# A streaming encoder layer on one core: down product's first operands loaded into the up stage's raw weight places, inverse roots issued in two parts, gate rows loaded further ahead

## The chip, the core and the metric

The kernel runs on one core of a Trainium2 chip. Five engines work side by side, each through its own queue in order: TensorE (PE, matmuls, with its weight loads as PEld), VectorE (DVE), ScalarE (ACT), GpSimd (POOL) and SyncE (SP). SP here only issues DMAs; POOL issues others, mostly those that add into memory. The metric is the device time of one execution in microseconds, the median of several runs.

## The reference, cut to what matters

One layer runs on 1024 prompt and 32 sample tokens (T = 1056) with width 1024. Between two mixing branches and the end stand the two parts in which the change lies:

```python
# ConvFFN: DFF = 2816
a, g = split(rms(x) @ w_up)
f    = (gelu(conv3(g)) * a) @ w_down
x    = x + rms(f) * g_post_ffn
# per-layer embedding
gate = sigmoid((rms(x) * g_pre_ple) @ w_ple_gate)
x    = x + rms(gate * (p @ w_ple)) * g_post_ple
```

## The kernel before, in words

Everything is kept transposed: features lie on the 128 partitions, tokens along the free axis. A product in nearly full fp32 is three matmuls in a reduced format: weights and rows are each split into a high part (an ACT copy, tiles `whi`, `d0` to `d8`, `eh`) and a low part (a DVE subtraction, `wlo`, the same `d` tiles, `el`), and hi·hi, hi·lo and lo·hi are added up.

**Up stage.** `up_strassen(f)` makes feature tile f (4 to 21) of the up product with seven half-size products (`mul`). It loads two raw weight tiles: one into the pool `wp` (tag `raw`, two places), one into the pool `sw` (tag `sraw`, two places). The pools `mp` and `sp` hold the normalised rows (`mh`, `ml`, and their sums `t1`, `t2`); `t3` lies in `sw`. For the last tile, f = 21, the final DVE steps are kept in a function `ends`, called later as `last_up[2]()`. `activate_steps` applies convolution and gelu and POOL writes the result to DRAM, `d_b`.

**Down product.** Seven products p, each of four output groups m; u = 4p + m counts groups from 0 to 27. One group is 11 tiles k of weights against rows, in three parts q (k 0 to 3, 4 to 7, 8 to 10), each k with two column halves and three matmuls: 66 matmuls. `row_load(p, i)` brings rows k = 2i and 2i+1 from `d_b` into a place `uraw` (three places), `row_split(p, i)` splits them into a `d` tile; `w_load(u)` brings a group's weights into a place `wraw` (two places), `w_split(u, q)` splits one part into `whi` and `wlo` (four places each). `uraw` and `wraw` are in the pool `rp`, which lies where `ml` was; the `d` tiles lie where `mh`, `ml` and the sums were. `gate_ahead` loads (into `raw`) and splits the gate's weights between the groups, from u = 4 on, and writes them to `d_gate`.

While products 5 and 6 run, `norm_first` does the norms of the first half of the tokens (`one`) in steps, at the places that `NORM_1` names: sums of squares, `inverse` (1/sqrt by ACT's Ln and Exp and one Newton step on DVE), `norm_rows`, and `norm_split`, which makes the gate's row tiles `eh` and `el`. `square_sum` gathers squares for the second half at the same time.

**Gate stage.** Products (c, n): c = 0 is the first half of the tokens in two column parts j, c = 1 and 2 are the quarters; n counts 8 output tiles. After each product's 24 matmuls ACT takes a sigmoid out of PSUM (`sig`), DVE multiplies it with a row of `d_pl` that SP has loaded into `plt` (L1759, L1769), ACT squares it, DVE adds the square up. `norm_second` does the second half's norms in steps at the places of `NORM_2`; `LAST` says where the last norm's total, sum, `inverse` and rows of quarters 0 and 1 stand. Each `inverse` needs another ACT function table than the sigmoid, so it is preceded and followed by an ACT_TABLE_LOAD. The last quarter's own norm follows all products: three pairs of matmuls with `onesM` (L1850), Ln, Exp, DVE, and the writes of `y`.

**What sets the order.** From the down product on PE, DVE and ACT keep the order in which the code is written (`manual_schedule`); what an engine waits for holds up all that stands behind it. SP's and POOL's queues are ordered by the scheduler, and an issue that waits for its place to be read holds up the issues behind it. The names with L are lines of the profile.

Of the kernel before, what the change touches and what calls it, by code (L numbers as in the profile page):

```python
# [112 lines left out]
def emit(tc, a):  # L113
# [1067 lines left out]

    def up_strassen(f):
        raw = [tl(wp, [P, KT, P], tag="raw", bufs=2), tl(wp, [P, KT, P], tag="raw", bufs=2) if f == UP_PLAIN else tl(sw, [P, KT, P], tag="sraw", bufs=2)]
# [48 lines left out]
        if f == FT - 1:  # L1232
# [6 lines left out]
            mul(Z, weight(s4, WL_ENG[5]), "b22", True, True)  # L1239
            ac.activation(c12, Z_, AF.Copy)  # L1240
# [9 lines left out]
            s3 = plus(a11, a21, ALU.subtract, WS_ENG[2])  # L1250
# [91 lines left out]
    def row_load(p, i):  # L1342
        if p < len(RSRC):
            n = 2 if i < 5 else 1
            raws[p, i] = tl(rp, [P, 2, HT], tag="uraw", bufs=3)[:, :n]
            dma.dma_start(raws[p, i], d_b[RSRC[p], 2 * i : 2 * i + n].rearrange("k p t -> p k t"))
# [36 lines left out]
    def w_load(u):  # L1383
        if u < NU:
            t = tl(rp, [P, HD * P], tag="wraw", bufs=2)
            dma.dma_start(t, WSRC[u // 4][u % 4])
            wraw[u] = t.rearrange("p (k c) -> p k c", c=P)

    def w_split(u, q):
        if u < NU:  # L1390
            raw, n = wraw[u][:, KS[q] : KS[q + 1]], KS[q + 1] - KS[q]
# [71 lines left out]
    def inverse(out, parts):  # L1463
# [5 lines left out]

        for ps, s in parts:  # L1470
            ac.activation(like(y, ps, s), ps, AF.Ln)
        ac.activation(y, y, AF.Exp, scale=-0.5)
        ve.tensor_tensor(t, y, y, op=ALU.mult)
        for ps, s in parts:
            ve.scalar_tensor_tensor(like(t, ps, s), like(t, ps, s), -0.5, ps, op0=ALU.mult, op1=ALU.mult)
        ve.scalar_tensor_tensor(out, t, 1.5, y, op0=ALU.add, op1=ALU.mult)
# [32 lines left out]
    def norm_split(s, rs, eh, el):  # L1509
        zs = pairs_of(s)  # L1510

        def low_half(i):
            ve.tensor_tensor(el[:, 2 * i : 2 * i + 2], zs[i], eh[:, 2 * i : 2 * i + 2], op=ALU.subtract)
# [8 lines left out]
        low_half(i)  # L1522
        yield
# [4 lines left out]
    def norm_first():  # L1528
# [5 lines left out]
        log_exp()  # L1534
        rs = tl(np_, [P, HT], tag="rs", bufs=1)
        inverse(rs, parts)
# [6 lines left out]
        log_exp()  # L1543
        rs = tl(np_, [P, HT], tag="rs", bufs=1)
        inverse(rs, parts)
# [5 lines left out]
    def norm_second():  # L1551
# [3 lines left out]
        log_exp()  # L1555
        rs = tl(np_, [P, HT], tag="rs", bufs=1)
        inverse(rs, parts)
        yield
# [7 lines left out]
        def tail(j, hl):  # L1566
            parts = own_sums(*hl)
            log_exp()
            r2 = tl(np_, [P, HC], tag="r2", bufs=1)
            inverse(r2, parts)  # L1570
            yield
# [34 lines left out]
    def gate_weights(n):  # L1606
# [8 lines left out]
        else:  # L1615
            if n < 4:
                t = [tl(rp, [P, HD * P], F32R, tag="wraw", bufs=2) if n == 2 else tl(rp, [P, 2, HT], F32R, tag="uraw", bufs=3).rearrange("p k t -> p (k t)") for x in range(2)]
# [20 lines left out]
    norm = None  # L1638
    for u in range(NU):
# [3 lines left out]
        for q in range(3):  # L1643
# [42 lines left out]
            if u == NU - 1 and q:  # L1686
                gate_weights(q - 1)
                gate_weights(q + 1)
            for i in range(NORM_1.get((p, m, q), 0)):
                next(norm, None)  # L1690
            if (p, m, q) in SQUARES_2:
# [3 lines left out]
                square_sum(acc[1], i, z[:, 4 + 2 * i : 6 + 2 * i, two])  # L1695
# [7 lines left out]
        if p == 6 and m % 2:  # L1703
            square_sum(acc[1], 2 + m // 2, z[:, m - 1 : m + 1, two])
# [4 lines left out]
        if (p, m) == (5, 3):  # L1709
            ub.release()  # L1710
    for i in norm:
        pass
# [19 lines left out]
    def last_inverse(c):  # L1732
        log_exp()
        w = SETS[c].stop - SETS[c].start
        rs = tl(np_, [P, HT], tag="rs", bufs=1)[:, :w]
        inverse(rs, sums[c])
# [212 lines left out]
```

## Time and profile before

| | us |
|---|---|
| median of 3 runs | 1987.55 |
| the runs | 1986.78 to 1989.57 |
| the profiled execution, its own time | 1986.21 |
| its span, first to last instruction | 1984.5 |
| PE busy in the span | 1929.8 (97%) |
| DVE busy | 1251.3 (63%) |
| ACT busy | 951.5 (48%) |
| POOL busy | 407.6 (21%) |
| granted TensorE clock, mean | 0.992 |

The profile is of one execution; times in it count from the span's start. A row of the timeline has start, duration, engine, line, operation, output<-input, shape and count, and in brackets how long the engine had been idle before and what ended that. A row of waits says which engine and line waited for which, the sum, the number of times and the longest. A row of windows has, for a stretch, its length, then each engine's busy time with its count of instructions (PE, PEld, DVE, ACT, POOL), the granted clock, the share of the DMA engines and their GB/s. In this trace the up stage ends and the down product begins near 1626, the gate stage begins near 1866, and the last gate product ends near 1961.5.

### The profile page before, as it was taken

Reading aid. Unit: us, or ns where it says so; the run is one execution under the profiler, and the core shown is the slowest. Engines: PE = TensorE matmul, PEld = TensorE weight load, DVE = VectorE, ACT = ScalarE, POOL = GpSimd, SP = SyncE. Lnnn points to the kernel's source line nnn. Section 1 sums busy time; section 2 is a strip of 40 time slices with the busy share of each in tenths; the row PEclk is TensorE's granted clock in tenths of the full one; section 3 lists DMA queues with packets and bytes.
Section 4 is the critical chain, followed back from the end, with each engine's and each line's share of the span. In section 5 each row is a group of like instructions: output and inputs, shape, how many; then the busy total and the mean of one; then the engine's idle time right before and its main releaser. Section 6 shows DMA issues by size and latency. Waiting matters only on the chain.

```text
span 1984.5 us, 34506 instructions
## 1 busy us (share of the span) xinstructions
PE 1929.8 (97%) x13594; PEld 1889.1 (95%) x13594; DVE 1251.3 (63%) x2546; ACT 951.5 (48%) x1747; POOL 407.6 (21%) x470
## 2 busy tenths in 40 slices
PE   8999999999999999998999999999999989999996
PEld 7999999999999999998999999999999989999995
DVE  7556556466376485466644676877677765558775
ACT  6356455454364553663423454434333344555554
POOL 4423322243122131111120121111112111001102
PEclk9999999999999999999999999999999999999998
DMA  7212211266235261337744256544445568887646
GB/s 281 68 56 75 72 56 57 71 173 176 85 105 143 92 170 60 107 107 234 277 132 136 89 160 214 174 130 136 130 114 119 115 172 281 271 289 245 224 124 107
DMA packets 106861, 289.04 MB, mean 146 GB/s; under 512 B 11652, under 2 KB 33868, under 8 KB 106060
## 3 DMA queue, kind: packets, MB, share of 16 engines
q1 hardware_dynamic: 78780, 198.45, 31.2%
q0 software_dynamic: 27632, 88.04, 16.3%
q8 instruction: 106, 1.74, 0.4%
q14 instruction: 55, 0.45, 0.1%
q10 hardware_dynamic: 288, 0.36, 0.1%
HBM read 198.49 MB, written 111.39 MB: 156 GB/s over the span
## 4 chain that ended last, share of the span: by engine, by line
PE 77%; DVE 12%; ACT 5%; DMA 4%; issue 3%; SPq 0%; POOL 0%; DVEq 0%; ACTq 0%
PE mm L228 13%; PE mm L229 13%; PE mm L230 13%; PE two L1209 6%; PE two L1211 6%; PE two L1210 6%; PE two L1652 2%; PE two L1651 2%; PE two L1650 2%; PE one L508 2%; PE two L730 2%; PE one L466 1%; DVE d L698 1%; DMA ev<-d_inv 1%; DMA uraw<-d_b 1%
## 5 line engine op out<-in xcount | busy, mean ns | idle before, releaser
L228 PE MATMUL mm<-xh,whi 128*128 128x352 f32 x1248 | 412.3, 330 | 0.0
L230 PE MATMUL mm<-xh,wlo 128*128 128x352 f32 x1248 | 412.1, 330 | 0.0
L229 PE MATMUL mm<-xl,whi 128*128 128x352 f32 x1248 | 410.0, 329 | 0.0
L208 POOL TENSOR_TENSOR wlo<-raw,whi 128x512 fp32r<-128x512 f32 x130 | 185.2, 1433 | 681.3 <-ACT whi L207 628.7
L228 PEld LDWEIGHTS mm<-xh,whi 128*128 128x128 f32 x1248 | 235.5, 189 | 1.6 <-DVE ev L352 0.5
L229 PEld LDWEIGHTS mm<-xl,whi 128*128 128x128 f32 x1248 | 235.2, 188 | 1.7 <-issue 0.3
L230 PEld LDWEIGHTS mm<-xh,wlo 128*128 128x128 f32 x1248 | 234.8, 188 | 1.1
L1650 PE MATMUL two<-d,whi 128*128 128x264 f32 x616 | 176.0, 286 | 4.2 <-ACT whi L1394 2.9
L1652 PE MATMUL two<-d,wlo 128*128 128x264 f32 x616 | 176.6, 287 | 2.1 <-DVE wlo L1395 2.0
L1651 PE MATMUL two<-d,whi 128*128 128x264 f32 x616 | 175.7, 285 | 2.9 <-DVE d L1354 2.9
L207 ACT ACTIVATE whi<-raw 128x512 fp32r<-128x512 f32 (+1 forms) x146 | 89.4, 621 | 157.0 <-PE mm L229 94.1
L1211 PE MATMUL two<-mh,wlo 128*128 128x264 f32 x576 | 163.1, 285 | 0.0
L1210 PE MATMUL two<-ml,whi 128*128 128x264 f32 x576 | 163.0, 284 | 0.0
L1209 PE MATMUL two<-mh,whi 128*128 128x264 f32 x576 | 161.4, 285 | 0.0
L1650 PEld LDWEIGHTS two<-d,whi 128*128 128x128 f32 x616 | 117.2, 190 | 5.3 <-ACT whi L1394 3.8
L1651 PEld LDWEIGHTS two<-d,whi 128*128 128x128 f32 x616 | 116.7, 189 | 3.6 <-DVE d L1354 3.6
L1652 PEld LDWEIGHTS two<-d,wlo 128*128 128x128 f32 x616 | 116.3, 189 | 3.2 <-DVE wlo L1395 3.2
L1210 PEld LDWEIGHTS two<-ml,whi 128*128 128x128 f32 x576 | 108.5, 188 | 0.0
L1211 PEld LDWEIGHTS two<-mh,wlo 128*128 128x128 f32 x576 | 108.5, 188 | 0.0
L1209 PEld LDWEIGHTS two<-mh,whi 128*128 128x128 f32 x576 | 107.4, 188 | 0.0
L352 DVE TENSOR_TENSOR ev<-mm,rstd 128x352 f32<-128x352 f32 x120 | 61.3, 517 | 54.5 <-PE mm L230 53.9
L1199 ACT ACTIVATE whi<-ws 128x512 fp32r<-128x512 f32 x72 | 45.4, 631 | 101.5 <-PE two L1210 76.2
(530 smaller groups left out, 5182.2 us busy)
## 6 DMA issues: line engine op xcount, KB each, us to landing
raw<-in_w_in SPq DMA_DIRECT2D x52, 512.0 KB, 4.1
uraw<-d_b SPq DMA_DIRECT2D x36, 528.0 KB, 4.6
d_b<-av POOLq DMA_DIRECT2D x33, 528.0 KB, 3.5
d_ws<-in_w_down POOLq DMA_DIRECT2D x24, 704.0 KB, 12.0
raw<-in_w_up SPq DMA_DIRECT2D x27, 512.0 KB, 3.7
wraw<-d_ws SPq DMA_DIRECT2D x16, 704.0 KB, 6.9
d_b<-gc POOLq DMA_DIRECT2D x11, 792.0 KB, 5.4
sraw<-in_w_up SPq DMA_DIRECT2D x17, 512.0 KB, 4.7
```

The costliest lines, as they stand in the source:

```text
L207: ac.activation(hi[-1][:, d], raw[:, b], AF.Copy)
L208: eng.tensor_tensor(lo[-1][:, d], raw[:, b], hi[-1][:, d], op=ALU.subtract)
L228: pe.matmul(ps, h, xh(kt), start=(first and i == 0), stop=False)
L229: pe.matmul(ps, h, xl(kt), start=False, stop=False)
L230: pe.matmul(ps, l, xh(kt), start=False, stop=(last and i == n - 1))
L352: return lambda ps, s: ve.tensor_tensor(t[:, s], ps, rstd(s), op=ALU.mult)
L1209: pe.matmul(ps[:, j, :HC], w[0][:, k], x[0][:, k, s], start=st, stop=False, skip_group_check=True)
L1210: pe.matmul(ps[:, j, :HC], w[0][:, k], x[1][:, k, s], start=False, stop=False, skip_group_check=True)
L1211: pe.matmul(ps[:, j, :HC], w[1][:, k], x[0][:, k, s], start=False, stop=sp_, skip_group_check=True)
L1650: pe.matmul(o, wh, xh_[:, s], start=(k == 0 and p in (0, 4, 5)), stop=False, skip_group_check=True)
L1651: pe.matmul(o, wh, xl_[:, s], start=False, stop=False, skip_group_check=True)
L1652: pe.matmul(o, wl, xh_[:, s], start=False, stop=(k == HD - 1 and p in (3, 4, 6)), skip_group_check=True)
```

## The change

- The first down weights, w_load(0), are loaded in two pieces into the two `raw` places, and the first two row loads, (0,0) and (0,1), into the two `sraw` places, which grow from 1024 to 1056 floats. Only rows from (0,2) on and weights from u = 1 on use `rp`. Rows (0,1) to (0,4) are all asked for ahead of the splits.
- `last_up[2]()` stands behind row_split(0,3) instead of ahead of it; the sum `s3` of the last up tile is written earlier.
- `inverse` gives back its DVE part as a function. In `norm_second` and for the last norm's quarters the ACT part is issued behind the step's sigmoid and the DVE part ahead of the next step; `norm_first` runs both at once as before.
- `norm_split` issues a pair's ACT copy ahead of the next pair's DVE products instead of behind its own; a pair of squares for the second half (`late`) is made one part later.
- The rows of `d_pl` are loaded by `pl_load`, one row ahead for c = 0 and three rows ahead for the quarters, behind the product that last read their place; a quarter's row uses a quarter of `plt`.
- `LAST` puts the quarters' totals, sums, roots and rows earlier.

```diff
+    def sw_raw():
+        return tl(sw, [P, 2 * HT], tag="sraw", bufs=2)
...
             mul(Z, weight(s4, WL_ENG[5]), "b22", True, True)
+            s3 = plus(a11, a21, ALU.subtract, WS_ENG[2])
...
-            raws[p, i] = tl(rp, [P, 2, HT], tag="uraw", bufs=3)[:, :n]
+            raws[p, i] = (sw_raw() if (p, i) < (0, 2) else tl(rp, [P, 2 * HT], tag="uraw", bufs=3)).rearrange("p (k t) -> p k t", k=2)[:, :n]
...
+            if u == 0:
+                ts = [tl(wp, [P, KT, P], tag="raw", bufs=2) for i in range(2)]
+                for i, t in enumerate(ts):
+                    n = (KT, HD - KT)[i]
+                    dma.dma_start(t[:, :n], src[:, KT * i : KT * i + n])
+                wraw[u] = [ts[0][:, : KS[1]], ts[0][:, KS[1] : KT], ts[1][:, : HD - KT]]
...
-        for i in range(KT // 2):
-            for j in range(2):
-                ve.scalar_tensor_tensor(zs[i][:, j], zs[i][:, j], col(G_PRE_PLE + 2 * i + j), rs, op0=ALU.mult, op1=ALU.mult)
-            ac.activation(eh[:, 2 * i : 2 * i + 2], zs[i], AF.Copy)
+        for i in range(KT // 2 + 1):
             if i:
-                low_half(i - 1)
+                ac.activation(eh[:, 2 * i - 2 : 2 * i], zs[i - 1], AF.Copy)
+            if i < KT // 2:
+                for j in range(2):
+                    ve.scalar_tensor_tensor(zs[i][:, j], zs[i][:, j], col(G_PRE_PLE + 2 * i + j), rs, op0=ALU.mult, op1=ALU.mult)
+            if i:
+                ve.tensor_tensor(el[:, 2 * i - 2 : 2 * i], zs[i - 1], eh[:, 2 * i - 2 : 2 * i], op=ALU.subtract)
             yield
...
         def tail(j, hl):
             parts = own_sums(*hl)
-            log_exp()
-            r2 = tl(np_, [P, HC], tag="r2", bufs=1)
-            inverse(r2, parts)
-            yield
+            r2, vs = tl(np_, [P, HC], tag="r2", bufs=1), []
+            yield lambda: vs.append(inverse(r2, parts))
+            vs.pop()()
...
     row_load(0, 0)
     w_load(0)
-    row_load(0, 1)
-    row_load(0, 2)
+    for i in range(1, 5):
+        row_load(0, i)
     for q in range(3):
         row_split(0, q)
-        row_load(0, 3 + q)
         w_split(0, q)
-    last_up[2]()
+    row_load(0, 5)
     row_split(0, 3)
     row_load(1, 0)
+    last_up[2]()
...
+            if late:
+                late_add = square_sum(acc[1], *late, True)
+                late = None
             for i in range(NORM_1.get((p, m, q), 0)):
                 next(norm, None)
+            if late_add:
+                late_add()
...
-    LAST = {(1, 5): [(last_total, 0)], (1, 7): [(last_sum, 0), (last_inverse, 0)], (2, 0): [(last_rows, 0, 0), (last_rows, 0, 2)], (2, 1): [(last_rows, 0, 4), (last_rows, 0, 6)],
-            (2, 2): [(last_total, 1)], (2, 4): [(last_sum, 1), (last_inverse, 1)]}
+    LAST = {(1, 4): [(last_total, 0)], (1, 6): [(last_sum, 0), (last_inverse, 0)], (1, 7): [(last_rows, 0, 0)],
+            (2, 0): [(last_total, 1)], (2, 1): [(last_rows, 0, 2)], (2, 2): [(last_sum, 1), (last_rows, 0, 4), (last_rows, 0, 6), (last_inverse, 1)]}
     for i in range(3):
-        LAST[2, 5 + i] = [(last_rows, 1, 2 * i)]
+        LAST[2, 3 + i] = [(last_rows, 1, 2 * i)]
...
+        if j == 0:
+            i = KT * c + n
+            while pl_rows and KT * pl_rows[0][0] + pl_rows[0][1] <= i + (3 if c else 1 + (n == KT - 1)):
+                pl_load(*pl_rows.pop(0))
+        while vs:
+            vs.pop()()
```

SP's queue at the end of the up stage, before. `uraw_17400`, `17404` and `17406` are the rows (0,0), (0,1) and (0,2), `17411`, `17420` and `17429` are (0,3) to (0,5), `17443` is (1,0); `wraw_17402`, `17476` and `17478` are the weights of u = 0, 1 and 2.

```order
L1371 DMA raw_17933<-in_w_ple_gate 128x1024
L1346 DMA uraw_17400<-d_b_12116 128x2x528
L1386 DMA wraw_17402<-in_w_down 128x1408
L1346 DMA uraw_17404<-d_b_12116 128x2x528
L1346 DMA uraw_17406<-d_b_12116 128x2x528
L1386 DMA wraw_17476<-in_w_down 128x1408
L1346 DMA uraw_17411<-d_b_12116 128x2x528
L1346 DMA uraw_17420<-d_b_12116 128x2x528
L1346 DMA uraw_17429<-d_b_12116 128x528
L1386 DMA wraw_17478<-in_w_down 128x1408
L1675 DMA out_o_conv<-convo_87 128x88
L1346 DMA uraw_17443<-d_b_12116 128x2x528
```

The same place in SP's queue after the change. `raw_17403` is the second piece of u = 0's weights (the first, `raw_17402`, stands just ahead), `sraw_17400` and `sraw_17406` are the rows (0,0) and (0,1), `uraw_17408` to `17412` are (0,2) to (0,4), `uraw_17435` is (0,5), `uraw_17440` is (1,0); `wraw_17478` and `17480` are the weights of u = 1 and 2.

```order
L1350 DMA sraw_17400<-d_b_12116 128x2x528
L1350 DMA sraw_17406<-d_b_12116 128x2x528
L1394 DMA raw_17403<-in_w_down 128x384
L1350 DMA uraw_17408<-d_b_12116 128x2x528
L1350 DMA uraw_17410<-d_b_12116 128x2x528
L1350 DMA uraw_17412<-d_b_12116 128x2x528
L1398 DMA wraw_17478<-in_w_down 128x1408
L1398 DMA wraw_17480<-in_w_down 128x1408
L1375 DMA raw_17933<-in_w_ple_gate 128x1024
L1350 DMA uraw_17435<-d_b_12116 128x528
L1375 DMA raw_17935<-in_w_ple_gate 128x1024
L1350 DMA uraw_17440<-d_b_12116 128x2x528
```

The two loads of gate weights moved from ahead of all of the down product's loads to either side of (0,5); (1,0) moved ahead of the write of `o_conv`.

ACT's queue in product 6, before. `wraw_19790` holds the weights of u = 26, `wraw_19884` those of u = 27; `sq` are squares for the second half.

```order
L1422 ACTIVATE sq_19909<-zd_17570 128x1056
L1394 ACTIVATE whi_19936<-wraw_19790 128x512
L1518 ACTIVATE eh_19943<-zd_17570 128x1056
L1394 ACTIVATE whi_19966<-wraw_19790 128x384
L1518 ACTIVATE eh_19943<-zd_17570 128x1056
L1422 ACTIVATE sq_19975<-zd_17570 128x1056
L1394 ACTIVATE whi_20002<-wraw_19884 128x512
L1518 ACTIVATE eh_19943<-zd_17570 128x1056
L1394 ACTIVATE whi_20034<-wraw_19884 128x512
L1518 ACTIVATE eh_19943<-zd_17570 128x1056
L1394 ACTIVATE whi_20060<-wraw_19884 128x384
```

After the change, the same place (`wraw_19792` is u = 26, `wraw_19885` u = 27):

```order
L1406 ACTIVATE whi_19935<-wraw_19792 128x512
L1434 ACTIVATE sq_19939<-zd_17572 128x1056
L1406 ACTIVATE whi_19967<-wraw_19792 128x384
L1534 ACTIVATE eh_19944<-zd_17572 128x1056
L1406 ACTIVATE whi_20000<-wraw_19885 128x512
L1434 ACTIVATE sq_20004<-zd_17572 128x1056
L1534 ACTIVATE eh_19944<-zd_17572 128x1056
L1406 ACTIVATE whi_20035<-wraw_19885 128x512
L1534 ACTIVATE eh_19944<-zd_17572 128x1056
L1406 ACTIVATE whi_20061<-wraw_19885 128x384
```

The weights' copies (`whi`) stand ahead of the copy to `eh` or the square that stood ahead of them; on DVE the squares' second addition moved from ahead of `wlo` of (27,0) to behind the third pair of `norm_split`.

ACT's queue in the last quarter, before: `sig_21176` is the sigmoid of (2,3), `sig_21208` of (2,4).

```order
L1839 ACTIVATE sig_21176<-mm_21177 128x264
L1772 ACTIVATE sig_21176<-zd_17570 128x264
L1754 ACTIVATE zd_17570<-zd_17570,vec_69 128x264
L237 ACT_TABLE_LOAD
L1471 ACTIVATE y_3071_21243<-one_21238 128x264
L1472 ACTIVATE y_3071_21243<-y_3071_21243 128x264
L1839 ACT_TABLE_LOAD
L1839 ACTIVATE sig_21208<-mm_21209 128x264
```

And after: `sig_21143` is the sigmoid of (2,2), `sig_21189` of (2,3).

```order
L1876 ACTIVATE sig_21143<-mm_21144 128x264
L237 ACT_TABLE_LOAD
L1486 ACTIVATE y_3068_21184<-one_21173 128x264
L1487 ACTIVATE y_3068_21184<-y_3068_21184 128x264
L1791 ACTIVATE sig_21143<-zd_17572 128x264
L1773 ACTIVATE zd_17572<-zd_17572,vec_69 128x264
L1876 ACT_TABLE_LOAD
L1876 ACTIVATE sig_21189<-mm_21190 128x264
```

The second quarter's root, with its two table loads, moved from ahead of the sigmoid of (2,4) to between those of (2,2) and (2,3).

More of the change, by code (lines that the diff above doesn't have):

```diff
@@ L1461, in own_sums, with inverse @@
         return out
-    def inverse(out, parts):
+    def inverse(out, parts, load=True):
         w = out.shape[-1]
@@ L1616, in gate_weights @@
             if n < 4:
-                t = [tl(rp, [P, HD * P], F32R, tag="wraw", bufs=2) if n == 2 else tl(rp, [P, 2, HT], F32R, tag="uraw", bufs=3).rearrange("p k t -> p (k t)") for x in range(2)]
+                t = [tl(rp, [P, HD * P], F32R, tag="wraw", bufs=2) if n == 2 else tl(rp, [P, 2 * HT], F32R, tag="uraw", bufs=3) for x in range(2)]
                 t = [v[:, : KT * P].rearrange("p (k c) -> p k c", c=P) for v in t]
@@ L1637, in emit @@
     done = 0
-    norm = None
+    norm = late = late_add = None
     for u in range(NU):
@@ L1694, in emit @@
                     acc[1] = tl(np_, [P, 2, HT], tag="acc", bufs=2)
-                square_sum(acc[1], i, z[:, 4 + 2 * i : 6 + 2 * i, two])
+                late = (i, z[:, 4 + 2 * i : 6 + 2 * i, two])
         down_out(p, m)
@@ L1703, in emit @@
         if p == 6 and m % 2:
-            square_sum(acc[1], 2 + m // 2, z[:, m - 1 : m + 1, two])
+            late = (2 + m // 2, z[:, m - 1 : m + 1, two])
         if (p, m) == (4, 3):
@@ L1710, in emit @@
             ub.release()
+    square_sum(acc[1], *late)
     for i in norm:
@@ L1808, in emit @@
                 for i in range(2):
+                    tgs[c, KT - 2 + i] = early[:, i]
+                for i in range(2):
                     kept.append(tl(np_, [P, 2, HT], tag="res", bufs=2)[:, :, :HC])
@@ L1811, in emit @@
         if j == 0:
-            if c < 2 or n < KT - 2:
-                tg[c] = plt[:, turn % 2, : s.stop - s.start]
-                turn += 1
-                dma.dma_start(tg[c], d_pl[n, :, s])
-            else:
-                tg[c] = early[:, n - KT + 2]
+            tg[c] = tgs.pop((c, n))
             sg = tl(gw, [P, HT], tag="sig", bufs=2)[:, : s.stop - s.start]
```

70 lines of the change are left out of this document (41 added, 29 removed).

## The prediction

> **What bounds the kernel now.** I read the windows first, since PE is busy for 97% of the span and the question is only where it is not.
>
> ```profile
> 1624.00:1632.00 8.00, 4.33 (x29) 3.50 (x28) 2.87 (x4) 2.99 (x4) 0.00 (x0) 1.00 1.05 352
> 1632.00:1640.00 8.00, 5.89 (x35) 5.46 (x36) 7.90 (x14) 5.65 (x8) 2.41 (x2) 0.86 0.67 215
> 1640.00:1648.00 8.00, 8.00 (x63) 8.00 (x63) 4.39 (x5) 1.50 (x2) 0.00 (x0) 0.93 0.90 291
> 1664.00:1850.00 186.00, 186.00 (x1536) 186.00 (x1535) 121.89 (x159) 101.89 (x152) 15.10 (x22) 1.00 0.82 262
> 1850.00:1862.00 12.00, 9.30 (x70) 8.46 (x70) 10.11 (x14) 4.45 (x6) 2.66 (x5) 1.00 0.29 75
> 1862.00:1961.00 99.00, 98.92 (x811) 98.54 (x811) 66.87 (x127) 53.26 (x97) 15.39 (x21) 1.00 0.59 170
> 1961.00:1984.50 23.50, 4.08 (x11) 1.81 (x9) 13.42 (x29) 7.99 (x16) 7.18 (x6) 0.59 0.63 92
> ```
>
> From 1664 to 1850 and from 1862 to 1961 PE is the bound: 811 matmuls in 99 us are 0.122 us each, so one group of 66 takes 8.05 us, a third of a group's first parts 2.9 us. PE is short of work in three places only: the start of the down product, product 6 near 1855, and the tail. The waits on PE from 1600 on name who ended them:
>
> ```profile
> PE two L1650 <- ACT whi L1394: 2.9, 2, 1.5
> PE two L1651 <- DVE d L1354: 2.9, 2, 2.0
> PE two L1652 <- DVE wlo L1395: 2.0, 4, 0.9
> ```
>
> The change touches all three places. I price them one by one and take the stretches between as they are.
>
> **Start of the down product.** Before, SP's loads stand behind PE's last read of `ml`:
>
> ```profile
> 1607.33 0.33 SPq L1371 DMA_DIRECT2D raw<-in_w_ple_gate  x1
> 1617.09 0.38 SPq L1346 DMA_DIRECT2D uraw<-d_b  x1
> 1621.41 1.09 ACT L1353 ACTIVATE d<-uraw 128x1056 fp32r<-128x1056 f32 x1 [3.58 <-DMA uraw<-d_b]
> 1626.64 0.63 ACT L1394 ACTIVATE whi<-wraw 128x512 fp32r<-128x512 f32 x1 [4.14 <-DMA wraw<-in_w_down]
> 1618.09 11.53 DMA uraw<-d_b
> 1627.32 0.39 PE L1650 MATMUL two<-d,whi 128*128 128x264 f32 x1 [1.37 <-ACT whi L1394]
> 1651.95 0.39 PE two L1652
> ```
>
> Rows (0,0) landed by 1621.41, the weights by 1626.64, rows (0,1) at 1618.09 + 11.53 = 1629.62. PE ended the up stage 1.37 us before 1627.32, at 1625.95. Two groups would end at 1625.95 + 16.1 = 1642.05; u = 2's third matmul came at 1651.95, so u = 2 began at 1651.7 in effect. The start costs 9.65 us, which no edit can exceed.
>
> After, weights u = 0 and rows (0,0) and (0,1) go to places that are free before 1607.33 (the gate load that took the last `raw` place was issued then), 18 us before they are needed: these three transfers leave the path. What is late next is DVE's queue, in the order of the rows:
>
> ```profile
> 1623.69 1.25 DVE L1354 TENSOR_TENSOR d<-uraw,d 128x1056 fp32r<-128x1056 f32 x1
> 1631.93 0.68 DVE L1395 TENSOR_TENSOR wlo<-wraw,whi 128x512 fp32r<-128x512 f32 x1
> 1634.17 0.70 DVE L1254 TENSOR_TENSOR c<-p,two 128x528 f32<-128x528 f32 x1
> 1636.25 0.18 DVE L1224 TENSOR_TENSOR gx<-c,two 128x32 f32<-128x32 f32 x1
> 1639.28 0.70 DVE L1354 TENSOR_TENSOR d<-uraw,d 128x528 fp32r<-128x528 f32 x1
> 1644.16 1.26 DVE L1351 SCALAR_TENSOR_TENSOR d<-uraw,d 128x1056 fp32r<-128x1056 f32 x1 [3.58 <-ACT d L1350]
> 1651.22 1.29 DVE L1395 TENSOR_TENSOR wlo<-wraw,whi 128x512 fp32r<-128x512 f32 x2
> ```
>
> DVE reaches `d0` at 1623.69 as before, behind the last up tile's steps. Then four row splits and three weight splits follow at steps of about 1.18 and 0.6 us, which ends `d3` at 1630.15; `last_up`'s five steps take 2.2 (1634.17 to 1636.4), so `d4` ends at 1633.55. PE starts at 1625.95 without a wait, reaches k = 8 at 1631.8 and waits 1.75 for `d4`; k = 8 and 9 end at 1635.0. For k = 10 it needs (0,5), whose load now stands behind the weights of u = 1 and 2 and one gate load: from 1617.1 SP moves three row loads of 528 KB, two weights of 704, 512 and 264, in all 3768 KB.
>
> ```profile
> uraw<-d_b SPq DMA_DIRECT2D x36, 528.0 KB, 4.6
> wraw<-in_w_down SPq DMA_DIRECT2D x12, 704.0 KB, 6.8
> raw<-in_w_up SPq DMA_DIRECT2D x27, 512.0 KB, 3.7
> ```
>
> The first 1760 KB landed by 1629.62 before, while POOL's writes of `d_b` ran too; for the other 2008 KB I take the 352 GB/s of the first window (344 KB/us): 1635.5. ACT's half copy and DVE's subtraction (0.64 estimated from the 0.70 beside it) end `d5` at 1636.8: 1.8 us of wait, and u = 0 ends at 1637.5. (1,0), behind another gate load, lands 1040 KB later, 1638.5; its ACT copy (1.09) lets DVE begin at 1639.6. Before, DVE took from 1644.16 to 1651.9 from there through the last up tile's activation to `wlo` of u = 2: 7.75 us, so 1647.3. PE wants it at 1637.5 + 8.05 + 0.24 = 1645.8 and waits 1.5; u = 2 begins at 1647.1. **Gain 4.6.** Bounds: with (0,5) early only `d4`'s 1.75 is left, gain 7.9; with (0,5) 3 us later and a clock drop, gain 1. I take the middle since its rates come from this very stretch. The earlier `s3` I cost at nothing: PE's seven products cover it in both versions.
>
> The drop: after its 2 us wait PE ran 3.4 us at half speed (clock 0.86 and 0.93 in the windows; 16 matmuls, 0.1 us more each):
>
> ```profile
> 1638.01 0.42 PE L1652 MATMUL two<-d,wlo 128*128 128x264 f32 x1
> 1638.23 0.42 PE L1650 MATMUL two<-d,whi 128*128 128x264 f32 x1
> ```
>
> My waits of 1.75, 1.8 and 1.5 are shorter and lie apart, and the window from 1850 with waits of 1.5 and 0.9 kept its clock of 1.00, so I count no drop; one would take 1.6 from the 4.6. [...]
>
> **Product 6.** Here ACT and DVE wait for one another in their fixed order:
>
> ```profile
> 1850.18 0.56 DVE L1395 TENSOR_TENSOR wlo<-wraw,whi 128x384 fp32r<-128x384 f32 x1 [1.57 <-ACT whi L1394]
> 1855.09 1.26 DVE L1428 TENSOR_TENSOR acc<-acc,sq 128x1056 f32<-128x1056 f32 x1 [1.21 <-ACT sq L1422]
> 1855.63 0.39 PE L1650 MATMUL two<-d,whi 128*128 128x264 f32 x1 [1.54 <-ACT whi L1394]
> 1857.01 0.39 PE L1652 MATMUL two<-d,wlo 128*128 128x264 f32 x1 [0.87 <-DVE wlo L1395]
> 1859.98 0.69 DVE L1395 TENSOR_TENSOR wlo<-wraw,whi 128x512 fp32r<-128x512 f32 x1 [0.51 <-ACT whi L1394]
> 1863.60 0.56 DVE L1395 TENSOR_TENSOR wlo<-wraw,whi 128x384 fp32r<-128x384 f32 x1 [0.40 <-ACT whi L1394]
> ```
>
> DVE's four waits for ACT make 3.7 us, and PE pays for them in u = 27, which should begin at 1853.9 and pays 1.54, 0.87 and, in the two later parts with their restarts, about 1.9: 4.3. In the new order ACT's `whi` stands ahead of the copy or square on which it waited, so these four waits go; the square's addition (1.2) moves behind the second `wlo` group's products. `wlo` (27,0) then ends near 1853, in time; (27,1) comes 3.3 earlier, done at 1857.4 against a need at 1857.0, and (27,2) 3.7 earlier, at 1860.45 against 1860.3. What is left is 0.6. **Gain 3.7**, at most 4.3; at least 1, if only the wait for the square goes.
>
> **The tail.**
>
> ```profile
> 1957.92 0.43 DVE L1769 TENSOR_TENSOR zd<-uraw,sig 128x264 f32<-128x264 f32 x1 [3.92 <-DMA uraw<-d_pl]
> 1961.25 0.28 PE L230 MATMUL mm<-eh,gw 128*128 128x264 f32 x1
> 1962.83 0.39 ACT L1839 ACTIVATE sig<-mm 128x264 f32<-128x264 f32 x1
> 1968.10 0.37 ACT L1839 ACTIVATE sig<-mm 128x264 f32<-128x264 f32 x1
> 1969.46 1.25 PE L1850 MATMUL one<-sig,onesM 128*128 128x264 f32 x2 [0.51 <-DVE sig L1774]
> ```
>
> PE's last product ends near 1961.5, but the last sigmoid comes at 1968.10: DVE stood 3.92 us for a row of `d_pl`, then ACT exchanged tables for the second quarter's root up to 1962.83, and five sigmoids followed at 1.75 us. With rows loaded three products (8.8 us) ahead the DMA wait goes; with the root behind (2,2) ACT has five products, 14.6 us, to work off the same lag at 1.75 per 2.9. I then get the last sigmoid at the product's end, 1961.6 to 1962, and the last pair of `onesM` 1.36 later as now (1969.46 - 1968.10), at 1963.3, since the two pairs ahead of it also take about 1 to 2 us from 1961.5. All that follows, Ln to the landing of `y`, moves along. **Gain 6.1**; at most 6.5 (last sigmoid at once), at least 3, if a lag as long as one table exchange and Ln, Exp is left. `last_rows(1, ...)` moves ahead with it and loads DVE with 0.9 per product beside 2.9 of PE. The other two-part roots put their table loads behind a sigmoid; six PSUM places (17 us) cover that.
>
> **The sum.** 4.6 + 3.7 + 6.1 = 14.4 on an execution of 1986.21 (span 1984.5 and 1.7 around it), 1971.8. The median of the runs is 1987.55, 1.3 above, so 1973.1 is my time. The lows, 1 + 1 + 3, give 1982.5; the highs, 7.9 + 4.3 + 6.5, 1968.9.
>
> **Rivals.**
> - The start stays bound by DMA. If SP goes on at the pace of its first 1760 KB, 141 KB/us from 1617.1, (0,5) lands at 1643.8, after 1637.3 of before, and the start loses some 3 us: 1987.55 + 3 - 9.8 = 1980.8. For it: DMA shares of 1.05, and the two gate loads now stand in this stretch; against it: POOL's writes end within it. Chance 0.15.
> - The start goes through: 7.9 + 4.3 + 6.5, 1968.9. The gate loads would have to cost nothing; 0.13.
> - ACT, not the rows, sets the tail: the table exchanges are as many as before, and the lag stays one exchange: 1976.2. Speaks against it that ACT is busy for only 53.3 of 99 us; 0.13.
> - The scheduler holds the early loads for something else and the start stays: 1977.7 at best, and with the tail too within 0.2%; 0.04 for the latter.
> - Slower: the roots' ACT part now waits for a sigmoid and a table load, so the last quarter's rows `el` come later. Before they end some 3 us before PE's use; each further us is a us of PE. It decides only from 3 + 14.4 + 4 = 21 us of lateness, and I find 2: 0.03, about 1991.5.
>
> **Numbers.** The forecast holds 0.52 (1970 to 1976). 0.2%, 4 us, is about what a measurement of this kernel tells from no change: faster 0.52 + 0.15 + 0.13 + 0.13 = 0.93, same 0.04, slower 0.03. The range reaches from 1968.5 to 1981.5, from the free start to the DMA-bound one.
>
> **What would show it.** Right: the first down matmul follows the up stage's without a gap; waits of 1 to 2 us for `d4` and `d5`; u = 27 with under 1 us of waits; no wait for `d_pl` near the end, and the last `onesM` pair within 2.5 us of the last product. Wrong: PE waiting for `d` rows by more than 4 us in u = 0 and 1, gaps in products 1 to 5 that were not there, or PE waiting at the start of (2,0).

## The result and the profile after

The changed kernel takes 1971.55 us (median of 4 runs, 1969.35 to 1973.61) against 1987.74 for the kernel before: ratio 0.9917, 95% interval 0.9900 to 0.9934. The forecast was 1973.1. The profiled execution took 1972.51, span 1970.8, 13.7 less than the 1984.5 of before.

I cut PE's work into stretches, from starts of matmuls in the trace, since the same matmuls run in both kernels:

| stretch, us | before | after | gain | forecast |
|---|---|---|---|---|
| span's start to the up stage's last matmul | 1625.67 | 1626.85 | -1.18 | 0 |
| start: from there to the first matmul of u = 4 | 42.16 | 36.49 | 5.67 | 4.6 |
| middle: u = 4 to the first of u = 24 | 161.15 | 161.15 | 0 | 0 |
| end of product 6: u = 24 to the last down matmul | 37.16 | 33.48 | 3.68 | 3.7 |
| gate: first gate matmul to the span's end | 118.19 | 112.71 | 5.48 | 6.1 |

The five rows make the 13.65 by which the spans differ. The medians differ by 16.2: the profiled execution of before was 1.5 us faster than the median, that of the kernel after 1.0 slower. The windows of the kernel after, read like those of before (length, then PE, PEld, DVE, ACT and POOL busy with counts, clock, DMA share, GB/s), show the start filled to 68 and 42 matmuls in its first two slices, where 29 and 35 stood:

```profile
1624.00:1632.00 8.00, 8.00 (x68) 8.00 (x67) 7.67 (x9) 2.71 (x3) 0.00 (x0) 1.00 1.06 348
1632.00:1640.00 8.00, 5.65 (x42) 5.03 (x42) 4.96 (x9) 4.42 (x6) 1.85 (x2) 1.00 0.98 341
1640.00:1648.00 8.00, 7.10 (x59) 6.88 (x58) 7.24 (x11) 4.50 (x8) 1.39 (x2) 1.00 0.88 298
1850.00:1862.00 12.00, 11.73 (x95) 11.48 (x95) 9.93 (x12) 4.00 (x5) 6.67 (x13) 1.00 0.75 196
```

What is left of waits on PE, from 1600 to the end:

```profile
PE two L1664 <- DVE d L1358: 2.0, 2, 1.6
PE two L1665 <- DVE wlo L1407: 1.2, 2, 0.9
PE one L1470 <- ACT y L1451: 0.7, 1, 0.7
PE one L1890 <- DVE sig L1793: 0.5, 1, 0.5
PE two L1663 <- ACT d L1357: 0.4, 1, 0.4
```

L1663 to L1665 are the down product's three matmuls (L1650 to L1652 before). In the timeline of the start, PE waits for `d4`, for both halves of `d5`, and for `wlo` of u = 2 (the last row), in the three places that were forecast:

```profile
1634.69 0.39 PE L1664 MATMUL two<-d,whi 128*128 128x264 f32 x1 [1.62 <-DVE d L1358]
1636.68 0.39 PE L1663 MATMUL two<-d,whi 128*128 128x264 f32 x1 [0.38 <-ACT d L1357]
1637.43 0.39 PE L1664 MATMUL two<-d,whi 128*128 128x264 f32 x1 [0.35 <-DVE d L1358]
1647.46 0.39 PE L1665 MATMUL two<-d,wlo 128*128 128x264 f32 x1 [0.90 <-DVE wlo L1407]
```

And the end, where the last sigmoid now follows the last product (1954.60) at once and the last pair of `onesM` (L1890) comes 1.7 us behind it, where it was 8.2:

```profile
1954.92 0.39 ACT L1876 ACTIVATE sig<-mm 128x264 f32<-128x264 f32 x1 [0.22 <-PE mm L230]
1954.60 0.28 PE L230 MATMUL mm<-eh,gw 128*128 128x264 f32 x1
1956.31 0.71 PE L1890 MATMUL one<-sig,onesM 128*128 128x264 f32 x2 [0.53 <-DVE sig L1793]
```

### The profile page after: what moved, and what is told of

Same layout as the page of the kernel before. It is cut to its first block, busy times and chain, and to the rows that moved or that the text cites. A ratio compares the mean times of both kernels' runs of the same rounds, so it can differ in the third digit from the quotient of the medians.

```text
span 1970.8 us, 34508 instructions
## 1 busy us (share of the span) xinstructions
PE 1924.6 (98%) x13594; PEld 1886.2 (96%) x13594; DVE 1251.5 (64%) x2546; ACT 951.2 (48%) x1747; POOL 405.4 (21%) x470
## 4 chain that ended last, share of the span: by engine, by line
PE 80%; DVE 10%; ACT 4%; DMA 3%; issue 2%; SPq 0%; DVEq 0%; ACTq 0%
PE mm L228 13%; PE mm L229 13%; PE mm L230 13%; PE two L1212 6%; PE two L1214 6%; PE two L1213 6%; PE two L1665 3%; PE two L1664 3%; PE two L1663 3%; PE one L508 2%; PE two L730 2%; PE one L466 1%; DVE d L698 1%; PE two L450 1%; PE one L744 1%
## 5 line engine op out<-in xcount | busy, mean ns | idle before, releaser
L1665 PE MATMUL two<-d,wlo 128*128 128x264 f32 x616 | 175.5, 285 | 1.2 <-DVE wlo L1407 1.2
L1663 PE MATMUL two<-d,whi 128*128 128x264 f32 x616 | 174.7, 284 | 0.4 <-ACT d L1357 0.4
L1665 PEld LDWEIGHTS two<-d,wlo 128*128 128x128 f32 x616 | 115.6, 188 | 1.6 <-DVE wlo L1407 1.6
L1663 PEld LDWEIGHTS two<-d,whi 128*128 128x128 f32 x616 | 116.4, 189 | 0.6 <-ACT d L1357 0.6
```

The source lines that it names most:

```text
L1663: pe.matmul(o, wh, xh_[:, s], start=(k == 0 and p in (0, 4, 5)), stop=False, skip_group_check=True)
L1665: pe.matmul(o, wl, xh_[:, s], start=False, stop=(k == HD - 1 and p in (3, 4, 6)), skip_group_check=True)
```

## The experiments

Each is read by the same stretches of its own profiled execution, where a stretch whose code is the same agrees between kernels to 0.1 us in product 6, 0.8 in the start and 0.9 in the gate stage, while the first stretch (up to the down product) wanders between 1624.1 and 1627.9. The stretches, us:

| kernel | start | middle | product 6 | gate |
|---|---|---|---|---|
| before | 42.16 | 161.15 | 37.16 | 118.19 |
| after | 36.49 | 161.15 | 33.48 | 112.71 |
| start_only | 36.37 | 161.15 | 37.19 | 118.53 |
| p6_only | 42.42 | 161.15 | 33.54 | 118.74 |
| tail_only | 42.99 | 161.15 | 37.17 | 112.49 |
| up_end_later | 36.51 | 161.15 | 33.46 | 112.64 |
| w0_in_wraw | 36.20 | 161.21 | 33.46 | 112.74 |
| no_dup | 36.37 | 161.15 | 33.46 | 112.23 |
| no_late | 36.48 | 161.15 | 34.42 | 113.09 |
| pl_two_places | 36.42 | 161.15 | 33.44 | 115.24 |
| last_places_before | 36.55 | 161.15 | 33.44 | 115.38 |
| start2_sum1 | 33.49 | 161.72 | 33.44 | 114.70 |
| start2 | 34.11 | 161.73 | 33.46 | 112.58 |
| start2_rows0 | 33.50 | 161.74 | 33.45 | 112.33 |

**Do the three parts add up?** The kernel before with one part of the diff each: start_only has the places and the order of the loads, splits, `last_up` and `s3`; p6_only has `norm_split` and `late`; tail_only has `inverse`, `LAST` and `pl_load`.

> Before, with only the part of the change at the down product's start (raw and sraw places, order of the loads and splits, earlier s3). Three stretches of PE are compared: from the last matmul of the up stage to the first of u = 4 (42.15 us before, 36.49 after the whole change), from the first of u = 24 to the last of the down product (37.15, 33.48), from the first gate product to the end of the span (118.19, 112.71). Theory (three parts that do not depend on each other): the first stretch becomes 36.5, the second and third stay at 37.2 and 118.2, total -5.7 us, about 1982.0. Rival (the parts depend on each other: what the start gains is partly lost later, or the later parts need the earlier start): the first stretch is the same but the second or third moves by over 0.5 us.

> Before, with only the new order in product 6 (ACT's copy of a pair issued ahead of the next pair's products, squares one part later). Theory: the second stretch goes from 37.15 to 33.5, the first stays at 42.2, the third at 118.2; total -3.7, about 1984.0. Rival (the copies were late because the whole stage ran late against its loads): the second stretch stays above 35.5.

> Before, with only the parts of the gate stage (root in two parts, rows of d_pl loaded further ahead, quarters' norm earlier). Theory: the third stretch goes from 118.19 to 112.7, the others stay at 42.2 and 37.2; total -5.5, about 1982.2. Rival: without the other parts the rows or weights of the gate stage stand differently, and the third stretch moves by over 0.5 us from 112.7.

Ratios to before: 0.9972 (0.9960 to 0.9983), 0.9988 (0.9979 to 0.9997) and 0.9971 (0.9959 to 0.9982). The medians fell by 6.2, 2.5 and 6.2 us, where 5.7, 3.7 and 5.5 were expected; the first stretch wanders by more than these differences. Each kernel moves its own stretch by 5.8, 3.6 and 5.7 us and leaves the others within 0.6, but for the start of tail_only, which has the old code and took 0.8 more. In all three the theory holds: the parts are independent.

**What holds the start after the change.** up_end_later moves one call:

```
-    last_up[2]()
     row_split(0, 4)
+    last_up[2]()
```

> After the change, with the last up tile's five DVE steps behind row_split(0,4) instead of ahead of it. Theory A (DVE's queue is what holds u = 0): the wait of 1.62 us for d4 goes, the first stretch falls from 36.49 to about 34.9, total -1.6, about 1970.0. Theory B (u = 0 ends with the landing of row (0,5), whose issue waits for the place that the split of (0,2) reads): the wait for d4 goes, but that for d5 grows from 0.7 to about 2.2, u = 1 begins 11.1 to 11.4 us after the first down matmul as before, and the time stays within 0.5 us of 1971.6.

Start 36.51, time 1972.72 (ratio 0.9931, 0.9916 to 0.9945): theory B, but for the time, which is 1.2 us above 1971.6 where it allowed 0.5 (half a microsecond of it was lost ahead of the down product in the profiled execution). The waits on PE say it, and ACT's timeline why: the wait moved from `d4` to `d5`, whose copy waits for the landing of row (0,5).

```profile
PE two L1663 <- ACT d L1357: 2.1, 1, 2.1
PE two L1665 <- DVE wlo L1407: 0.9, 1, 0.9
PE two L1664 <- DVE d L1358: 0.4, 1, 0.4
```

```profile
1636.45 0.64 ACT L1357 ACTIVATE d<-uraw 128x528 fp32r<-128x528 f32 x1 [2.99 <-DMA uraw<-d_b]
```

So u = 0 ends with (0,5). The start as a whole ends elsewhere: the last wait of PE in it, 0.9 for `wlo` of u = 2, is left in both kernels. On DVE this `wlo` stands behind the split of row (1,0) and the last up tile's activation, and ACT's copy of (1,0) waits for that row's landing, before:

```profile
1643.04 1.09 ACT L1350 ACTIVATE d<-uraw 128x1056 fp32r<-128x1056 f32 x1 [3.37 <-DMA uraw<-d_b]
1651.95 0.39 PE L1652 MATMUL two<-d,wlo 128*128 128x264 f32 x1 [0.71 <-DVE wlo L1395]
```

and after (the matmul that waits for this `wlo` is the one at 1647.46 shown above):

```profile
1638.54 1.09 ACT L1354 ACTIVATE d<-uraw 128x1056 fp32r<-128x1056 f32 x1 [0.23 <-DMA uraw<-d_b]
```

From the copy of (1,0) to this matmul it takes 8.91 us before, 8.92 after and 8.92 in up_end_later (1639.10 to 1648.02), and from there to u = 4 15.88 in all three. Counted from the up stage's last matmul, the copy begins at 17.37 before, at 11.69 after: these 5.7 us are the whole gain of the start. Before, (1,0) was issued at 1639.39, after it at 1631.33. Even with (0,5) there in time, theory A's 1.6 us would have been lost again at this `wlo`.

**Which places carry the start.** w0_in_wraw leaves the weights of u = 0 where they were:

```
-            if u == 0:
+            if u < 0:
                 ts = [tl(wp, [P, KT, P], tag="raw", bufs=2) for i in range(2)]
```

> After the change, but the weights of u = 0 go into a wraw place as before, which is free only when PE has read ml for the last time; the first two rows stay in sraw places. The two gate loads then go ahead of the down product's loads again. Theory R (the rows' places carry the start's gain): the weights are first in the queue and land near 1623, (0,5) is no longer behind a gate load, and the first stretch is 35.5 to 36.7. Theory W (the weights' place carries part): the first down matmul comes over 1 us after the up stage's last and the first stretch is 37.5 or more.

Start 36.20, time 1971.84 (ratio 0.9920, 0.9891 to 0.9949): theory R. The weights are first in SP's queue at 1616.68 and ACT splits them at 1621.81, ahead of PE's 1625.38. Below are rows of DVE, SP and ACT around (0,5) and, last, ACT's copy of (1,0), first of w0_in_wraw:

```profile
1586.46 0.33 SPq L1375 DMA_DIRECT2D raw<-in_w_ple_gate  x1
1606.92 0.35 SPq L1375 DMA_DIRECT2D raw<-in_w_ple_gate  x1
...
1628.33 1.26 DVE L1358 TENSOR_TENSOR d<-uraw,d 128x1056 fp32r<-128x1056 f32 x1 [1.43 <-ACT d L1357]
1629.61 0.33 SPq L1350 DMA_DIRECT2D uraw<-d_b  x1
...
1633.01 0.64 ACT L1357 ACTIVATE d<-uraw 128x528 fp32r<-128x528 f32 x1
1636.67 1.09 ACT L1354 ACTIVATE d<-uraw 128x1056 fp32r<-128x1056 f32 x1 [1.01 <-DMA uraw<-d_b]
```

then of the kernel after:

```profile
1628.40 1.25 DVE L1358 TENSOR_TENSOR d<-uraw,d 128x1056 fp32r<-128x1056 f32 x1
1628.52 0.33 SPq L1375 DMA_DIRECT2D raw<-in_w_ple_gate  x1
1629.69 0.33 SPq L1350 DMA_DIRECT2D uraw<-d_b  x1
...
1635.99 0.64 ACT L1357 ACTIVATE d<-uraw 128x528 fp32r<-128x528 f32 x1 [3.04 <-DMA uraw<-d_b]
```

In both, (0,5) is issued 0.02 to 0.04 us behind the end of DVE's split of (0,2) (1628.33 + 1.26 and 1628.40 + 1.25), which last reads its place. With the gate load ahead of it, it is there after 6.3 us (1635.99), without it after at most 3.4 (1633.01). The two executions have different bases, though: counted from the up stage's last matmul (1625.26 and 1626.85), (0,5) is issued 1.5 us later in w0_in_wraw, since (0,2) lands behind the weights there, and is taken up 1.4 us earlier. What PE waits for changes with it:

```profile
PE two L1664 <- DVE d L1358: 2.8, 3, 1.6
```

These are waits for `d2`, `d3` and `d4`, and none for `d5`. Counted in the same way, u = 1 begins at 11.95 in w0_in_wraw and at 11.29 after: the weights' places do bring u = 0 forward by 0.7 us. But in both PE takes up the third matmul of u = 2 8.92 us behind the copy of (1,0), and this copy begins at 11.41 in w0_in_wraw, where no gate load is left in this stretch, and at 11.69 after. So the weights' places add nothing to the start beside those of the rows. The weights' places without those of the rows, and the rows' places without the new order of loads and splits, have no run.

**The duplicate load.** Before and after both load the rows (1,1) twice. no_dup leaves the second out:

```
                 row_split(p, 5)
-                row_load(p + 1, 1)
+                if p:
+                    row_load(p + 1, 1)
```

> After the change, without the second of two loads of the same rows (1,1) that before and after both issue while u = 1 runs (528 KB). Theory: no wait of PE in the first stretch goes back to a transfer behind it, so the stretch stays within 0.3 us of 36.5. Rival (DMA traffic still bounds the start): it falls by 1 us or more.

Start 36.37, time 1971.02 (ratio 0.9918, 0.9900 to 0.9936): nothing waited for it. This rules out the duplicate alone: the landing of (1,0), issued ahead of it, does bound the start, as shown above.

**The squares in product 6.** no_late makes them where they stood:

```
-                late = (i, z[:, 4 + 2 * i : 6 + 2 * i, two])
+                square_sum(acc[1], i, z[:, 4 + 2 * i : 6 + 2 * i, two])
...
-            late = (2 + m // 2, z[:, m - 1 : m + 1, two])
+            square_sum(acc[1], 2 + m // 2, z[:, m - 1 : m + 1, two])
```

> After the change, but the pairs of squares are made at their old places (ahead of the next part's steps, not one part later). Theory (as predicted): DVE waits for ACT's square again by about 1.2 us ahead of wlo of (27,0), and the second stretch rises from 33.5 to 34.5 or 35. Rival 1: the order of norm_split alone does it, 33.5. Rival 2: the squares are the main part, 36 or more.

34.42, just below what the theory gave and well above its first rival; time 1972.40 (ratio 0.9923, 0.9894 to 0.9952). DVE waits for ACT's square again, and PE pays once, for `wlo` of (27,0):

```profile
1847.31 1.26 DVE L1440 TENSOR_TENSOR acc<-acc,sq 128x1056 f32<-128x1056 f32 x1 [1.21 <-ACT sq L1434]
1848.49 0.68 DVE L1407 TENSOR_TENSOR wlo<-wraw,whi 128x512 fp32r<-128x512 f32 x1
```

```profile
PE two L1665 <- DVE wlo L1407: 0.9, 1, 0.9
```

So 0.9 of the 3.7 is the squares; the rest, 2.7, falls by difference to the order in `norm_split`.

**Rows or root in the tail.** One undoes the rows' early loading, the other the places of the quarters' norm:

```
-        i = n % (2 * HT // w)
+        i = n % 2
...
-            while pl_rows and ... <= i + (3 if c else 1 + (n == KT - 1)):
+            while pl_rows and ... <= i + 1 + (n == KT - 1 and c == 0):
```

> After the change, but a quarter's row of d_pl has two places instead of four and is asked for one product ahead, as before; roots and LAST stay as changed. Theory R (the rows' late loading is what cost the tail): DVE waits for d_pl again by 3 to 4 us in the last products, the last sigmoid comes later, and the third stretch rises from 112.7 to 115 or more. Theory A (the place of the second quarter's root among ACT's sigmoids is what cost it): waits for d_pl come back but the stretch stays within 0.7 us of 112.7, since the root is done four products ahead of the end.

```
-    LAST = {(1, 4): [(last_total, 0)], ... (2, 2): [(last_sum, 1), ..., (last_inverse, 1)]}
+    LAST = {(1, 5): [(last_total, 0)], ... (2, 4): [(last_sum, 1), (last_inverse, 1)]}
```

> After the change, but with the old table LAST (totals, sums, roots and rows of the quarters at their old places, the second root at (2,4)); rows of d_pl are loaded three ahead as changed. Theory R: with the rows there in time ACT has worked off its lag before the root, so the third stretch stays within 1 us of 112.7. Theory A: the root at (2,4) pushes the last sigmoids behind the last product as before, the last one comes over 3 us after it, and the stretch is 116 or more.

115.24 and 115.38 (times 1975.13 and 1974.14; ratios 0.9939, 0.9917 to 0.9962, and 0.9934, 0.9912 to 0.9957). The first lands where theory R put it; the second refutes R (at most 113.7) and misses A (116) as well. Neither was the whole: each costs 2.5 to 2.7 us alone. Before, start_only and p6_only, with both undone, show 5.5 to 6.0; there `inverse` is in one part again as well, which no run undoes by itself. In pl_two_places two waits for rows come back at the end of DVE's queue:

```profile
1951.01 0.43 DVE L1788 TENSOR_TENSOR zd<-uraw,sig 128x264 f32<-128x264 f32 x1 [1.68 <-DMA uraw<-d_pl]
1954.21 0.43 DVE L1788 TENSOR_TENSOR zd<-uraw,sig 128x264 f32<-128x264 f32 x1 [1.62 <-DMA uraw<-d_pl]
```

In last_places_before no row is late, but the second root's table loads stand between the last sigmoids, which follow 1.75 us apart up to 2.7 us behind the last product (1953.64):

```profile
1948.49 1.28 ACT L237 ACT_TABLE_LOAD   x1
1951.52 1.28 ACT L1875 ACT_TABLE_LOAD   x1
1952.81 0.39 ACT L1875 ACTIVATE sig<-mm 128x264 f32<-128x264 f32 x1
1954.58 0.37 ACT L1875 ACTIVATE sig<-mm 128x264 f32<-128x264 f32 x1
1956.33 0.37 ACT L1875 ACTIVATE sig<-mm 128x264 f32<-128x264 f32 x1
```

**A faster version.** The three waits left in the start and the one at (2,2) gave the next kernels. start2 (in all three):

```
 # w_load(0): (0,5) into the rest of the second raw place
+                raws[0, 5] = ts[1].rearrange("p k c -> p (k c)")[:, P * (HD - KT) : P * (HD - KT) + HT].unsqueeze(1)
+                dma.dma_start(raws[0, 5], d_b[RSRC[0], 10:11].rearrange("k p t -> p k t"))
...
     row_split(0, 3)
     row_load(1, 0)
-    last_up[2]()
     row_split(0, 4)
-    row_load(1, 1)
+    row_split(0, 5)
...
-            w_split(u + 1, q)
-            i = ROW_AT.get((m, q))
+            for at in {(0, 0): [(1, 0), (1, 1)], (0, 1): [], (0, 2): [(1, 2), (2, 0)], (1, 0): []}.get((u, q), [(u + 1, q)]):
+                w_split(*at)
+            if (u, q) == (0, 0):
+                last_up[2]()
+            i = 0 if (u, q) == (1, 0) else None if (u, q) == (0, 1) else ROW_AT.get((m, q))
```

start2_sum1 also moves `(last_sum, 1), (last_inverse, 1)` from (2,2) to (2,3) and the rows behind it by one; start2_rows0 instead moves `(last_rows, 0, 0)` from (1,7) to (2,0).

> After the change, with two more changes meant to be faster. Start: (0,5) is loaded into the unused rest of the second raw place (384 of 1024 floats hold weights), early; all rows of product 0 are split ahead of the last up tile's end; the weights' splits of u = 1 and the first of u = 2 stand ahead of that tile's activation; row (1,0) is split behind them; the second load of row (1,1), which the program issues twice, is left out. Tail: the second quarter's sum and root move from (2,2) to (2,3), its rows with them. Theory (u = 0 waits only for d4, the landing of (0,5), and wlo of u = 2): the first stretch falls from 36.5 to 32.3 to 33.5 (four groups alone are 32.2). Rival (what is late next takes it: wlo of u = 1 behind DVE's splits, or weights of u = 2 and 3): 34.5 or more. Third stretch: if PE's wait of 0.7 for the sum is all that (2,2) cost, 112.7 falls to 111.5; if a root one product later pushes the last sigmoids, it stays at 112.5 to 113.5. Total by the theory -4 to -5 from 1971.6, about 1967.

> The start of start2_sum1 (first stretch 33.49 there, 36.49 after the change), with the quarters' norm left at the places of the changed kernel (third stretch 112.7). Theory (the stretches do not depend on each other): 33.5, 33.5 and 112.2 to 113.1; between the first and second 161.2 to 161.7, since PE now waits for the weights of u = 4; total about 2.5 us below the changed kernel, 1969. Rival (the start's gain is given back later): the middle part or the third stretch grows by more than 1 us.

> As start2, with the first two rows of quarter 0's norm, last_rows(0, 0), moved from (1,7) to (2,0), behind last_total(1). Theory: these two DVE steps (1.44 us) are what makes PE wait 0.71 us for the sum's rows at (2,2) and restart late (1.2 us in all), so that wait goes and the third stretch falls by about 1.2, to 111.5. Rival: DVE, which is full for the next 6 us, hands the 1.4 us on to the second quarter's root and the last sigmoids, and the stretch stays at 112.7 or rises up to 114.

start2: 1969.13 (ratio 0.9902, 0.9885 to 0.9918); start2_rows0: 1968.05, the lowest of all (0.9901, 0.9886 to 0.9916); start2_sum1: 1971.06 (0.9919, 0.9905 to 0.9932). The intervals overlap with that of the changed kernel, so that none is shown to be faster in time; start2_sum1 missed its 1967 by 4 us. The stretches say what they gain. The start falls to 33.5 to 34.1, 2.4 to 3.0 less; the middle grows by 0.6. What is late next is the weights of u = 4, read from `d_ws`. PE's wait for them stands at the first matmul of u = 4 and so counts to the start; it is 1.3 us in start2 and 0.5 to 0.7 in the other two, which accounts for the 0.6 us between their starts (waits on PE in start2, and ACT's copy):

```profile
PE two L1663 <- ACT whi L1408: 1.3, 1, 1.3
```

```profile
1659.86 1.15 ACT L1408 ACTIVATE whi<-wraw 128x512 fp32r<-128x512 f32 x2 [7.95 <-DMA wraw<-d_ws]
```

The tail gave nothing. With the sum one product later PE's products take 95.04 us instead of 96.50, but the last sigmoid comes 3.0 us behind the last product (1954.76 against 1951.75) and the stretch rises by 2.0, beyond what either expected. With the two rows later PE's products take 95.17 instead of the 96.31 of start2 and what follows them 17.16 instead of 16.27: of the 1.2 us expected 0.25 is left, which is less than this stretch wanders. What PE gains there it waits for later, since DVE's squares for the `onesM` matmuls come no earlier (0.5 in start2):

```profile
PE one L1894 <- DVE sig L1797: 1.3, 2, 1.1
```

## Why the prediction was right

- **The start, 4.6 forecast, 5.67 measured.** The mechanism was right: no wait ahead of u = 0, then waits for `d4` (1.75 forecast, 1.62 in the row), `d5` and `wlo` of u = 2 (1.5 forecast, 0.9), and u = 2 held by the steps behind row (1,0). The mis-sized term is the landing of the rows in SP's queue. I let (1,0) land at 1638.5, which on this execution's base, 1.18 later, is 1639.7; ACT took it up at 1638.54. This 1.1 us is the difference between forecast and gain, as the 7.75 us from DVE's split of (1,0) to the end of that `wlo` came out (1639.66 to 1647.4). (0,5), by the same rate, was there 0.7 us ahead of my time, and the wait for `d5` was 0.38 + 0.35 where 1.8 was forecast; for the start that made no difference. The step "these three transfers leave the path" held, but was needed for the rows only: w0_in_wraw gained 5.96 without the weights' places.
- **The start's bounds.** The upper one, 7.9 if (0,5) came early, left out that `wlo` of u = 2 stands behind (1,0) and not behind (0,5). start2, which also splits the first weights of u = 2 ahead of (1,0), reached 8.1 to 8.7 below before in this stretch. The lower one, 1, does not come out of its terms: 4.6 - 3 - 1.6 is 0. The rival that DMA goes on at its old pace had (0,5) land at 1643.8; ACT took it up at 1635.99.
- **No clock drop** was counted, and none came: 1.00 in all three windows. That says little, since p6_only ran the old start, with waits as long, without a drop as well, and no run shows that a drop there costs the 1.6 us of the prediction.
- **Product 6, 3.7 forecast, 3.68 measured.** DVE's four waits for ACT, 3.7 us, are gone (0.2 for `eh` is left), and 0.3 on PE is left where 0.6 was forecast.
- **The tail, 6.1 forecast, 5.48 measured.** From the last product to the end it gained 7.0 (23.21 to 16.20). The step that failed is to "take the stretches between as they are": PE's products themselves took 1.5 us longer (94.98 to 96.50). At the sum of the second quarter, now at (2,2), PE waits for ACT's copy of the total of squares, whose last addition stands on DVE behind rows of quarter 0. The timeline of PE, L1470 being the sum's matmul:

```profile
1938.34 0.28 PE L230 MATMUL mm<-eh,wraw 128*128 128x264 f32 x1
1939.34 0.39 PE L1470 MATMUL one<-y,onesDr 128*128 128x264 f32 x1 [0.71 <-ACT y L1451]
1940.04 0.29 PE L228 MATMUL mm<-eh,uraw 128*128 128x264 f32 x1
```

  I had priced `LAST`'s earlier places for DVE and ACT, not for PE, whose queue they stand in too. start2_rows0, where these rows stand behind the total, has no such wait. The place is not the only cause, though: in last_places_before, with the sum at its old place (2,4), PE waits as well, and there no run shows why:

```profile
1944.35 0.39 PE L1470 MATMUL one<-y,onesDr 128*128 128x264 f32 x1 [1.01 <-ACT y L1451]
```

  The rival that only ACT sets the tail gave 1976.2; the runs show that the quarters' places and the rows carry about half each.
- **The sum.** The profiled execution after lost 1.18 us before the down product, and had lost it by 50 us, where both kernels run the same code. Without it the sum 14.4 stands against 14.83. That these lie so near is in part luck: the start gave 1.1 more than forecast and the tail 0.6 less.

## What to carry to other kernels

Where a stage starts behind another, look for places that the earlier stage has already left, for the operands that are needed first, and follow what would have been loaded there: here the weights' new place pushed two later loads into the busiest microseconds (issued at 1628.52 and 1630.16, DMA share 1.06 from 1624 to 1632) and gained nothing beside the rows' (start 36.49 us with it, 36.20 without). Of several waits in a row, look for the one that ends last and follow it back: here the wait for `d4` was the longest, 1.62 us, and yet the landing of row (1,0) alone set the start's gain (taken up 5.7 us earlier, the start 5.67 shorter). When two waits lie on top of one another (the DVE steps and the landing of a row; a late row and a table exchange), taking one away gave nothing or half here (36.51 us against 36.49 in up_end_later; either one undone cost 2.5 to 2.7 of the tail's 5.48), so list all that is due at that point before pricing one. A step that is moved earlier stands in every engine's queue, the matmul engine's too, and there it can make all that follows wait for its inputs (0.71 us at the sum of the second quarter).

## What the runs showed of the hardware

- The half-rate stretch in the start of before (matmuls 0.22 us apart from 1638.01 to 1641.09, 0.12 behind it) is not fixed by the code. tail_only and p6_only run the same start as before, and PE's first three long waits are much the same (1.2 to 1.8, 1.1 to 1.4 and 0.9 us); the one of 2.0 us comes in before and p6_only only. In windows from 1632 to 1640 us the granted clock was 0.86 in before, 0.67 in tail_only and 1.00 in p6_only:

```profile
1632.00:1640.00 8.00, 8.00 (x46) 7.76 (x46) 7.44 (x12) 4.64 (x7) 2.41 (x2) 0.67 0.63 202
```

```profile
1632.00:1640.00 8.00, 5.02 (x34) 4.39 (x35) 7.90 (x12) 6.02 (x8) 2.37 (x2) 1.00 0.78 263
```

  The first is tail_only, the second p6_only, whose start took 42.42, no less than the 42.16 of before with its drop: there the drop cost nothing that shows, as `wlo` of u = 2 was late anyway (PE waited 0.71 us for it in before). tail_only took 42.99, with ACT's copy of (1,0) 0.8 us later than before; whether its drop has part in that is open. PE's longest wait ahead of the drop was 2.0 us in before and 1.4 us in tail_only; p6_only waited 2.0 us too and kept its 1.00.
- Executions differ before the change comes to bear. Ahead of the down product the profiled ones differ by up to 3.9 us (1624.07 in start_only, 1627.93 in start2_sum1) with nearly the same code. Part of such differences arises in the first 50 us. From 25 to 50 us the clock was 0.93 in before and 0.86 in after, and PE had 100 matmuls there instead of 111; at 47 us the kernel after was 1.35 us behind:

```profile
25.00:50.00 25.00, 20.89 (x111) 17.22 (x110) 21.84 (x23) 13.06 (x22) 14.57 (x10) 0.93 0.60 222
```

```profile
25.00:50.00 25.00, 19.93 (x100) 15.96 (x98) 19.50 (x19) 12.15 (x20) 13.03 (x9) 0.86 0.60 219
```

  The first is before, the second after. Between start_only and start2_sum1, where the clock was 0.93 in this window in both, only 0.4 of the 3.9 us stands at 100 us, by the starts of the same matmuls; the rest comes in steps near 740, 900 to 920 and 975 us. From 900 to 950 us the clock was 0.97 in start_only and 0.90 in start2_sum1. Whether the lower clock or the waits between the matmuls make these delays is open.
